# Splitting pooled columns into high and low parts: both copies of a bank before both subtracts, and a tile laid out by token

## The chip, the cores and the metric

One Trainium2 chip (trn2), one of its cores. The metric is the device time of one execution in microseconds, as the median of several runs. TensorE does the matrix products, ScalarE (ACT) copies and functions, VectorE (DVE) arithmetic on tiles, GpSimd (POOL) small odd work, SyncE (SP) issues most transfers. All of them run their own instruction lists in order and wait for one another by semaphores. PSUM, into which TensorE writes, has eight banks of 128 partitions x 512 fp32.

## The reference, cut to what matters

One layer of a trunk over 1024 latent tokens of width 1024, with 256 context tokens, all fp32. The normed and modulated tokens h are multiplied by one input projection, whose columns feed a gated linear attention and a pooling mixer. The pooling mixer takes 512 columns p = h @ w_in[:, 1568:2080], in four groups of 128 columns, group g with its own window w of 2, 4, 8 or 16 on the 16 x 64 grid of tokens:

```python
m = window_mean(window_mean(xg2, w, 2), w, 1).reshape(B, L, POOL_GROUP)
outs.append(m - xg)
y = jnp.einsum('blgc,gcd->blgd', y, w_pool)
```

Attention and pooling are joined, projected out and added to the stream; then comes a mixture of 32 experts (top group, top two of its experts), and a last norm.

## The kernel before, in words

The kernel keeps fp32 accuracy with products in the faster fp32r type: an operand is split into a high part (a ScalarE copy that rounds it to fp32r) and a low part (a VectorE subtract, operand minus high part). The helper `split` (line 196) issues these two; its copy shows as L197 and its subtract as L198 in the profile, for all operands, so the tile tells which one it is. A product is then three matmuls: high x high, high x low, low x high.

The first phase (lines 302 to 553) loads the tokens, norms and transposes them (`x_sq`, `x_rs`, `x_scale`, `x_T`: the transposes of TensorE are L332, into a bank, and ScalarE and VectorE copy half of them each to `hall`, L338 and L336), works out the modulation from `w_ada`, and computes the pooled columns. `prep` (line 395) splits a slice of `hall` into `phh` and `phl`; `wp_split` the weights into `wph` and `wpl`; `pool_mm` (line 403) adds the three products of one slice k, over four or two token tiles, into PSUM banks, one bank of 512 pooled columns for each token tile (L407, L408, L410). There are three sets of banks: `accA`, token tiles 0 to 3; `accB`, tiles 4 and 5; `accC`, tiles 6 and 7, computed in a second pass over k. When a set is complete, `pool_out` (line 412) takes its banks to SBUF: for each bank and each half m of its columns (groups 0 and 1, then 2 and 3) one split, that is one copy and one subtract of 128 partitions x 256 columns, into `pparts[m]`. The names of the profile for these tiles are `mix` and `bank`: `mix<-bank` at L197 and L198 are pool_out's instructions, eight of each for accA, four each for accB and accC.

After accA is out come the last product steps of accB, the transposes of the two context tiles (`x_T(8)`, `x_T(9)`, which use the banks of accA's first two tiles and two others), pool_out of accB, and then accC's products, among which stand `prep`, the splits of the gate weights (`wg_steps`: transfers at L249 into the two buffers `wraw`, `wgh` and `wgl`), and `row_step` (L290, sums over rows of `w_ada` that are brought into `wat`).

The order of instructions on TensorE, VectorE and ScalarE in this phase is the program's (a manual schedule); instructions from behind the phase are placed between them by the framework's scheduler, which works from its own model of time. It also derives all waits: from tiles that overlap, and from PSUM banks.

Behind the phase `box_sums` (line 559) sums over the windows on TensorE: for each group, token tile s and part j one weight tile `pparts[g // 2][:, g % 2, j, s]` (128 x 128) against constant box tables, which come through `wraw` (L601) and are rounded by ScalarE (L603, names `wvl` and `wvh`); its matmuls are L583. `box_means` (L593) scales the sums. Then follow the projections, the attention, the output projection, the router and the experts.

Of the kernel before, what the change touches and what calls it, by code (L numbers as in the profile page):

```python
# [8 lines left out]
F32 = mybir.dt.float32  # L9
F32R = mybir.dt.float32r  # L10
# [3 lines left out]
AF = mybir.ActivationFunctionType  # L14
OP = mybir.AluOpType
# [4 lines left out]
P = 128  # L20
D = 1024
NT = 8
# [110 lines left out]
def hybrid_layer(ctx, tc, x, c, ctx_in, c_ctx, w_ada, b_ada, norm1_g, w_in, w_decay, b_decay, gla_norm_g,  # L133
                 w_pool, pool_scale, w_out, norm2_g, w_rg, w_re, w_e_in, w_e_out, final_g, cst_d, inv_d, out):
    nc = tc.nc
    ve, sc, gp, te, sy = nc.vector, nc.scalar, nc.gpsimd, nc.tensor, nc.sync
# [59 lines left out]
    def split(hi, lo, src, en=ve):  # L196
        sc.activation(hi, src, AF.Copy)  # L197
        en.tensor_tensor(lo, src, hi.bitcast(F32), OP.subtract)  # L198
# [4 lines left out]
    def bank(*banks):  # L203

        turn[banks] = (turn.get(banks, -1) + 1) % len(banks)
        b = banks[turn[banks]]
        return ps.tile([P, 512], F32, name=f"bank{b}", tag=f"bank{b}")
# [12 lines left out]

    mixp = ExitStack()
    mp = mixp.enter_context(tc.tile_pool(name="mixp", bufs=1))
    pparts = [mp.tile([P, 2, 2, NT, P], F32R, name=f"mix{j}", tag=f"mix{j}") for j in range(2)]
    mixs, pcol = {}, []

    def mix_half(j):
# [75 lines left out]
    with tc.tile_pool(name="pp", bufs=2) as pp, \  # L302
# [109 lines left out]
        def pool_out(acc, half, js):  # L412
            for j in js:
                i = 4 * half + j
                for m in range(2):
                    src = acc[j][:, m * 256:(m + 1) * 256].rearrange("p (g c) -> p g c", g=2)
                    split(pparts[m][:, :, 0, i], pparts[m][:, :, 1, i], src)

        x_load(0)
        sy.dma_start(ident, cst_d[:, 0:P])  # L420
# [77 lines left out]
        for kp in range(1, 4):  # L498
# [18 lines left out]
            if kp < 3:  # L517
                prep(0, 2 * kp + 2, sc)
            else:
                pool_out(accA, 0, g4)  # L520
                prep(1, 0)
# [11 lines left out]
        x_T(8, xb)  # L533
        x_T(9, xb)
        pool_out(accB, 1, g2)
        for k in range(8):
            affine(gp, k, 1024, 1280, 1)
# [5 lines left out]
        for k in range(8):  # L543
            pool_mm(accC, 1, k, range(2, 4))
            if k < 6:
                prep(1, k + 2)
            if k in (0, 2, 4, 5):
                wg_steps[(0, 2, 4, 5).index(k)]()
            if k == 7:
                pool_out(accC, 1, range(2, 4))  # L550
            if k < 4:
                row_step()
            if k == 6:
                ada_end(7, racc, 2)
# [4 lines left out]
    def box_sums(g, box):  # L559

        down, up = BOX_REACH[g]
        tab, at = BOX_AT[g]
        accs = []
        for half in range(2):
            acc = bank(2, 3, 6, 7)
            accs.append(acc)
            todo = []
            for s in range(4 * half, 4 * half + 4):
                n = BOX_C0[g] + BOX_C[g][s]
                todo.append((s, box[2 + n // 8][:, n % 8 * P:(n % 8 + 1) * P], s, s))  # L570
            for s in range(NT):
                lo, hi = max(s - down, 4 * half), min(s + up, 4 * half + 3)
                if lo > hi:
                    continue
                near = lo - s + down
                if g == 3 and near:
                    near = 1 if hi - s < up else 6 - (hi - lo + 1)
                o = at + near * P
                todo.append((s, box[tab][:, o:o + (hi - lo + 1) * P], lo, hi))
            for n, (s, rhs, lo, hi) in enumerate(todo):  # L580
                dst = acc[:, (lo - 4 * half) * P:(hi + 1 - 4 * half) * P]
                for j in range(2):
                    te.matmul(dst, lhsT=pparts[g // 2][:, g % 2, j, s], rhs=rhs, start=(n + j == 0),  # L583
                              stop=(n == len(todo) - 1 and j == 1))
        return accs

# [33 lines left out]
    for i in range(NT):  # L620
        hs = tile_split(i)
        pg = bank(0, 1, 4)
        tokproj(pg, hs, wg)
        gs = (gpool.tile([P, 512], F32, name="gs") if i < NT - 1 else
              wst.tile([P, D], F32, name="wraw", tag="wraw", bufs=2)[:, 0:512])
        with tc.manual_schedule(engines={mybir.EngineType.Activation}):
            sc.activation(gs, pg, AF.Silu)
            if i == NT - 1:
                sc.preload_act_table_set("natural_log_exp_and_others")
        ve.tensor_tensor(gs.rearrange("p (h d) -> p h d", h=H), gs.rearrange("p (h d) -> p h d", h=H),  # L630
                         gnb[:, None, :].to_broadcast([P, H, P]), OP.mult)
        sy.dma_start(g_d[i], gs)
        if i < 7:
            for k in ((0,), (1,), (2,), (3,), (4,), (5,), (6, 7))[i]:
                ada_sum(ada_acc, 3, k)
        else:
            ada_end(5, ada_acc, 3)
        if i < 4:
            sums_g[3 - i] = box_sums(3 - i, box)
        if i == 1:  # L640
            at = mix_half(1).rearrange("p i k n -> p (i k n)")
            pcol.extend(at[:, g * D:(g + 1) * D] for g in range(4))
            box_means(3, sums_g[3])
        if 1 <= i < 4:
            box_means(3 - i, sums_g[3 - i])
        (ka_steps if i < 4 else v_steps)[i % 4]()
# [38 lines left out]
    with tc.tile_pool(name="kv", bufs=2) as kv:  # L685
# [115 lines left out]
        with tc.manual_schedule(engines={mybir.EngineType.PE}):  # L801
            k_proj(0, range(8))
            decay_in(0)
            for n in range(10):
                c = 3 if n else 6
# [513 lines left out]
    with tc.manual_schedule(engines={mybir.EngineType.PE, mybir.EngineType.DVE}):  # L1319
# [39 lines left out]
        i = NT - 1  # L1359
# [432 lines left out]
    with tc.manual_schedule(engines={mybir.EngineType.PE, mybir.EngineType.Pool, mybir.EngineType.DVE,  # L1792
# [20 lines left out]
        m = last.m  # L1813
# [105 lines left out]
```

## Time and profile before

| what | us |
|---|---|
| median of three runs | 847.03 |
| the three runs | 845.0, 847.03, 853.17 |
| the profiled execution's own time | 848.0 |
| its span in the profile | 845.9 |

The profile is of one execution. Times in rows are microseconds from the start of its span, and durations in nanoseconds where marked so. PE is TensorE's matmuls, PEld its weight loads, which overlap them; the ends of matmuls are modelled, so they are spaced more closely than their durations. A row of the timeline gives the start, the length from first start to last end, the engine, line, operation, the tile written and the tiles read, the shape and how many such instructions are merged in it; in brackets the idle time of the engine just before it and what ended that.

### The profile page before, as it was taken

To read this page: it belongs to the slowest core of one execution; us is meant where nothing else is said; L and a number is where in the kernel's file an instruction comes from. 1 tells how busy PE (TensorE), PEld (TensorE's weight loads), DVE (VectorE), ACT (ScalarE), POOL (GpSimd) and SP (SyncE) were. 2 spreads that over 40 slices of the span, in tenths; PEclk is the share of its full clock that TensorE was granted. 3 is DMA by queue.
4 is the path that set the end of the run, shared out by engine and by line. 5 is a ranking of instruction groups with operands and counts; after the bars stand their busy time and mean duration, and the time that the engine had idled before them with its cause. 6 is when DMAs were issued, how large, how long until landed. Compare 5 with 4: busy or idle time off the path is not lost. (4 is left out here: it accounts for less than half of the span.)

```text
span 845.9 us, 11767 instructions
## 1 busy us (share of the span) xinstructions
PE 742.8 (88%) x4078; PEld 502.2 (59%) x4078; DVE 428.5 (51%) x884; ACT 276.7 (33%) x525; POOL 211.1 (25%) x201
## 2 busy tenths in 40 slices
PE   4897989999999997889999564999999999997573
PEld 3675778878888985768888452434444433342232
DVE  4547856457786796754465876144223212121136
ACT  4675542344544556344443221111100101010023
POOL 2222000000000203444148655022223321221113
PEclk9999999999999998989999695899998999999688
DMA  9975774163352338564477668999999999999665
GB/s 322 300 265 175 251 255 175 58 192 131 111 171 75 138 107 311 170 200 149 138 248 240 227 217 280 289 368 370 388 349 367 348 321 351 375 357 364 205 221 200
DMA packets 78253, 206.84 MB, mean 245 GB/s; under 512 B 12515, under 2 KB 24919, under 8 KB 78193
## 3 DMA queue, kind: packets, MB, share of 16 engines
q1 hardware_dynamic: 70816, 185.45, 61.8%
q0 software_dynamic: 6624, 18.51, 9.0%
q10 hardware_dynamic: 752, 2.11, 0.9%
q8 instruction: 33, 0.54, 0.3%
q14 instruction: 28, 0.22, 0.1%
HBM read 179.68 MB, written 29.50 MB: 247 GB/s over the span
## 5 line engine op out<-in xcount | busy, mean ns | idle before, releaser
L1677 POOL DMA_INDIRECT x_d<-y,idx x30 | 43.0, 1434 | 161.5 <-DMA x_d<-y,idx 116.0
L1664 DVE SCALAR_TENSOR_TENSOR y<-bank,wtab,gtm 128x512 f32<-128x512 f32 (+1 forms) x40 | 29.5, 749 | 81.3 <-DMA x_d<-y,idx 53.5
L270 PE MATMUL bank<-woh,hh 128*128 128x512 f32 x124 | 53.3, 430 | 0.0
L271 PE MATMUL bank<-wol,hh 128*128 128x512 f32 x124 | 50.9, 410 | 0.7 <-DVE wol L198 0.7
L272 PE MATMUL bank<-woh,hl 128*128 128x512 f32 x124 | 50.8, 409 | 0.1
L1650 ACT ACTIVATE gT<-bank 128x256 f32<-128x256 f32 (+1 forms) x20 | 7.4, 376 | 132.6 <-PE bank L1648 132.6
L1624 DVE COPY hh<-bank 128x512 f32<-128x512 f32 (+1 forms) x20 | 13.4, 670 | 68.8 <-PE bank L1620 68.6
L270 PE MATMUL bank<-wkh,hh 128*128 128x288 f32 (+1 forms) x144 | 42.9, 298 | 0.0
L272 PE MATMUL bank<-wkh,hl 128*128 128x288 f32 (+1 forms) x144 | 42.0, 292 | 0.1
L271 PE MATMUL bank<-wkl,hh 128*128 128x288 f32 (+1 forms) x144 | 41.9, 291 | 0.0
L1635 PE MATMUL bank<-hall,hh 128*32 128x512 f32 (+4 forms) x156 | 40.9, 611 | 0.0
L1599 POOL DMA_INDIRECT hall<-h_d,idx x32 | 31.5, 983 | 37.2 <-PE bank L1620 28.5
L198 POOL TENSOR_TENSOR wkl<-wraw,wkh 128x512 fp32r<-128x512 f32 x4 | 6.2, 1555 | 135.1 <-ACT wkh L197 135.1
L197 ACT ACTIVATE hh<-hall 128x1024 fp32r<-128x1024 f32 x26 | 27.4, 1054 | 37.3 <-PE bank L271 33.2
L198 DVE TENSOR_TENSOR hl<-hall,hh 128x1024 fp32r<-128x1024 f32 x26 | 31.6, 1222 | 14.3 <-ACT hh L197 14.2
L1635 PE MATMUL bank<-mix,hh 128*64 128x512 f32 (+3 forms) x132 | 37.7, 600 | 0.0
L1635 PE MATMUL bank<-dS,hh 128*32 128x512 f32 (+3 forms) x88 | 37.2, 640 | 0.0
L270 PE MATMUL bank<-wvh,hh 128*128 128x512 f32 x80 | 32.0, 400 | 0.0
L271 PE MATMUL bank<-wvl,hh 128*128 128x512 f32 x80 | 31.8, 397 | 0.0
L272 PE MATMUL bank<-wvh,hl 128*128 128x512 f32 x80 | 31.6, 395 | 0.0
L1642 DVE TENSOR_TENSOR ga<-ga,bank 128x256 f32<-128x256 f32 (+1 forms) x20 | 8.4, 420 | 45.3 <-ACT ga L1641 45.2
L1620 PEld LDWEIGHTS bank<-ident,hall 128*128 128x128 f32 (+1 forms) x160 | 22.3, 211 | 15.0 <-issue 15.0
(467 smaller groups left out, 1945.5 us busy)
## 6 DMA issues: line engine op xcount, KB each, us to landing
hall<-in_w_expert_in_dram SPq DMA_DIRECT2D x25, 512.0 KB
mix<-in_w_expert_in_dram SPq DMA_DIRECT2D x25, 512.0 KB
wat<-in_w_ada_dram SPq DMA_DIRECT2D x24, 512.0 KB
dS<-in_w_expert_in_dram SPq DMA_DIRECT2D x18, 512.0 KB
wraw<-in_w_ada_dram SPq DMA_DIRECT2D x16, 512.0 KB
woh<-in_w_expert_in_dram SPq DMA_DIRECT2D x13, 512.0 KB
wraw<-in_w_in_dram SPq DMA_DIRECT2D x12, 512.0 KB
wol<-in_w_expert_in_dram SPq DMA_DIRECT2D x11, 512.0 KB
```

What stands on the lines that cost most here:

```text
L197: sc.activation(hi, src, AF.Copy)
L198: en.tensor_tensor(lo, src, hi.bitcast(F32), OP.subtract)
L270: te.matmul(dst, lhsT=ah[k], rhs=bh[k], start=(k == ends[0]), stop=False)
L271: te.matmul(dst, lhsT=ah[k], rhs=bl[k], start=False, stop=False)
L272: te.matmul(dst, lhsT=al[k], rhs=bh[k], start=False, stop=(k == ends[1]))
L1599: gp.indirect_dma_start(out=self.xg[q], out_offset=None, in_=h2_d, in_offset=ix, bounds_check=D - 1, oob_is_err=False)
L1620: te.transpose(pt[:, j * m:(j + 1) * m], self.xg[:, k // 2 * 256 + k % 2:(k // 2 + 1) * 256:2], ident[0:m, 0:m])
L1624: ve.tensor_copy(self.xT[:, 4:8], pt)
L1635: te.matmul(self.ph[q], lhsT=self.xT[:, k, q], rhs=w[:, j * 512:(j + 1) * 512], start=(k == 0), stop=(k == 7))
L1642: ve.tensor_tensor(ga, ga, self.ph[0:m, 256:512], OP.mult)
L1664: ve.scalar_tensor_tensor(y[:, ns], py[n][0:m], self.wt, gtm[0:m, ns], op0=OP.mult, op1=OP.mult)
L1677: gp.indirect_dma_start(out=x2_d, out_offset=ix, in_=y[q], in_offset=None, bounds_check=D - 1, oob_is_err=False, compute_op=OP.add)
```

## The change

For each bank, `pool_out` now issues the copies of both halves first and the subtracts of both halves after them; before, it went copy, subtract, copy, subtract. The tile `pparts[m]` is laid out by token tile, then part (high, low), then group, where it was group, part, token tile; `box_sums` takes its weight tiles at the new place. Sizes, types and the number of instructions are the same.

```diff
-    pparts = [mp.tile([P, 2, 2, NT, P], F32R, name=f"mix{j}", tag=f"mix{j}") for j in range(2)]
+    pparts = [mp.tile([P, NT, 2, 2, P], F32R, name=f"mix{j}", tag=f"mix{j}") for j in range(2)]
...
         def pool_out(acc, half, js):
             for j in js:
                 i = 4 * half + j
+                src = [acc[j][:, m * 256:(m + 1) * 256].rearrange("p (g c) -> p g c", g=2) for m in range(2)]
                 for m in range(2):
-                    src = acc[j][:, m * 256:(m + 1) * 256].rearrange("p (g c) -> p g c", g=2)
-                    split(pparts[m][:, :, 0, i], pparts[m][:, :, 1, i], src)
+                    sc.activation(pparts[m][:, i, 0], src[m], AF.Copy)
+                for m in range(2):
+                    ve.tensor_tensor(pparts[m][:, i, 1], src[m], pparts[m][:, i, 0].bitcast(F32), OP.subtract)
...
-                    te.matmul(dst, lhsT=pparts[g // 2][:, g % 2, j, s], rhs=rhs, start=(n + j == 0),
+                    te.matmul(dst, lhsT=pparts[g // 2][:, s, j, g % 2], rhs=rhs, start=(n + j == 0),
```

## Rows read from the trace of the kernel before

**Rows 1.** The page's first part: busy time, share of the span and instructions of each engine.
```profile
PE 742.8 (88%) x4078; PEld 502.2 (59%) x4078; DVE 428.5 (51%) x884; ACT 276.7 (33%) x525; POOL 211.1 (25%) x201
```

**Rows 2.** The table by stage. Columns: stretch and its length, then busy time and instructions of PE, PEld, DVE, ACT and POOL, the granted clock of TensorE (1.00 is full speed), the busy share of the 16 DMA engines, GB/s.
```profile
73.70:86.00 12.30, 8.24 (x35) 6.07 (x36) 9.14 (x20) 7.97 (x19) 4.46 (x8) 0.86 0.18 64
86.00:98.00 12.00, 12.00 (x58) 9.19 (x57) 11.36 (x13) 4.85 (x7) 0.00 (x0) 1.00 0.82 267
98.00:109.00 11.00, 9.58 (x42) 7.45 (x41) 7.22 (x13) 8.42 (x13) 0.62 (x1) 1.00 0.73 238
109.00:130.00 21.00, 19.18 (x102) 16.55 (x103) 13.48 (x15) 6.37 (x8) 0.00 (x0) 0.92 0.86 278
...
200.00:250.00 50.00, 49.93 (x306) 44.15 (x306) 40.14 (x81) 24.57 (x53) 0.00 (x0) 1.00 0.44 148
```

**Rows 3.** The waits in the stretch 73.7 to 86 us: who waited for whom, us in total, times, longest.
```profile
ACT mix L197 <- DVE mix L198: 9.3, 6, 5.5
...
PE bank L332 <- DVE mix L198: 2.5, 2, 1.9
...
DVE mix L198 <- ACT mix L197: 2.2, 5, 0.5
PE bank L407 <- ACT phh L197: 2.0, 2, 1.6
```

**Rows 4.** The timeline of 66 to 76 us, on ScalarE, VectorE and TensorE.
```profile
68.36 0.37 ACT L197 ACTIVATE mix<-bank 128x256 fp32r<-128x256 f32 x1
...
69.21 1.28 DVE L290 SCALAR_TENSOR_TENSOR racc<-wat,cT,racc 128x1024 f32<-128x1024 f32 x1 [1.76 <-DMA wat<-in_w_ada_dram]
...
73.75 0.42 DVE L198 TENSOR_TENSOR mix<-bank,mix 128x256 fp32r<-128x256 f32 x1
74.20 0.66 ACT L197 ACTIVATE mix<-bank 128x256 fp32r<-128x256 f32 x2 [5.47 <-DVE mix L198]
74.62 0.76 DVE L198 TENSOR_TENSOR mix<-bank,mix 128x256 fp32r<-128x256 f32 x2 [0.45 <-ACT mix L197]
75.19 0.63 PE L332 MATMUL bank<-ident,xs 128*128 128x128 f32 x4 [1.91 <-DVE mix L198]
```

**Rows 5.** The timeline of 75 to 90.5 us, on the same engines.
```profile
75.41 0.66 ACT L197 ACTIVATE mix<-bank 128x256 fp32r<-128x256 f32 x2 [0.55 <-DVE mix L198]
...
76.39 2.03 PE L332 MATMUL bank<-ident,xs 128*128 128x128 f32 x12 [0.58 <-DVE mix L198]
...
78.60 0.48 DVE L606 MEMSET gs<- 128x512 f32 x1 [0.82 <-PE bank L332]
78.77 0.80 PE L407 MATMUL bank<-wph,phh 128*128 128x512 f32 x1 [0.34 <-ACT phh L197]
79.00 0.36 DVE L198 TENSOR_TENSOR mix<-bank,mix 128x256 fp32r<-128x256 f32 x1
...
80.64 0.64 PE L410 MATMUL bank<-wph,phl 128*128 128x512 f32 x2
81.11 0.39 PE L407 MATMUL bank<-wph,phh 128*128 128x512 f32 x1
...
81.68 0.41 DVE L198 TENSOR_TENSOR mix<-bank,mix 128x256 fp32r<-128x256 f32 x1
...
83.74 0.42 DVE L198 TENSOR_TENSOR mix<-bank,mix 128x256 fp32r<-128x256 f32 x1 [0.45 <-ACT mix L197]
...
84.28 0.50 PE L407 MATMUL bank<-wph,phh 128*128 128x512 f32 x1 [1.65 <-ACT phh L197]
...
85.37 0.73 PE L410 MATMUL bank<-wph,phl 128*128 128x512 f32 x2
```

**Rows 6.** Instructions by tile and by line, with the least, median and largest duration in ns, first and last start in us, and the shapes: pool_out's copies and subtracts; the copy of line 711 and, below it, what it waited for (us, times); the VectorE sum of line 298.
```profile
L197 ACT ACTIVATE mix<-bank x16: 366/384/392, 68.4 to 101.5; 128x256 fp32r<-128x256 f32 x16
L198 DVE TENSOR_TENSOR mix<-bank,mix x16: 361/416/425, 73.8 to 102.8; 128x256 fp32r<-128x256 f32 x16
...
L711 ACT ACTIVATE kvb<-bank x10: 365/384/385, 172.0 to 280.7; 128x256 f32<-128x256 f32 x10
...
  DVE aext L710: 7.6, 8
...
L298 DVE TENSOR_TENSOR bg<-bank,bg x1: 417/417/417, 98.3 to 98.3; 128x256 f32<-128x256 f32 x1
```

**Rows 7.** The timeline of 75 to 90.5 and 90 to 104 us, the gate weights' instructions on VectorE, ScalarE and SyncE's queue (SPq).
```profile
85.24 1.21 DVE L198 TENSOR_TENSOR wgl<-wraw,wgh 128x1024 fp32r<-128x1024 f32 x1
...
86.48 0.39 SPq L249 DMA_DIRECT2D wraw<-in_w_in_dram  x1
...
89.97 1.21 DVE L198 TENSOR_TENSOR wgl<-wraw,wgh 128x1024 fp32r<-128x1024 f32 x1
90.07 1.06 ACT L197 ACTIVATE wgh<-wraw 128x1024 fp32r<-128x1024 f32 x1 [1.86 <-DMA wraw<-in_w_in_dram]
...
91.21 0.38 SPq L249 DMA_DIRECT2D wraw<-in_w_in_dram  x1
...
96.06 1.06 ACT L197 ACTIVATE wgh<-wraw 128x1024 fp32r<-128x1024 f32 x1 [4.40 <-DMA wraw<-in_w_in_dram]
```

**Rows 8.** The timeline of 104 to 150 us, TensorE's first box sums.
```profile
108.92 1.00 PE L583 MATMUL bank<-wvl,mix 128*128 128x128 f32 x7 [1.42 <-ACT wvl L603]
...
110.74 6.26 PE L583 MATMUL bank<-wvl,mix 128*128 128x128 f32 x28 [0.82 <-ACT wvl L603]
```

## The prediction

> **What bounds the kernel now.** I read first the busy line of the page: TensorE is busy for 742.8 of 845.9 us [rows 1], so the end can only come earlier where TensorE stands idle, or runs slowly, and gets something for it. Next the table by stage [rows 2]. The stretch 73.7 to 86.0 us is the poor one: TensorE busy 8.24 of 12.30 us at a granted clock of 0.86, VectorE 9.14, the DMA engines at a share of 0.18. That is the stage in which the first two sets of pooled banks are split. Behind it TensorE is full in 86 to 98 and (49.93 of 50) in 200 to 250; between lie shorter gaps at 98 to 109 and 109 to 130. A microsecond saved in the poor stretch therefore shifts full work, and stays saved unless one of the two later gaps grows by it.
>
> Then the waits of that stretch [rows 3]. ScalarE's copies waited 9.3 us, six times, for VectorE's subtract, at most 5.5 us in one go; VectorE waited 2.2 us in five waits for ScalarE's copy; TensorE waited 2.5 us for the subtract (a bank that a transpose wants) and 2.0 us for ScalarE's high part of the next operand.
>
> Last the order of time. I call A0, A1 the copies of a bank's two high parts (groups 0 and 1, then 2 and 3) and S0, S1 the subtracts for its low parts. A0 of the first bank runs at 68.36, then ScalarE does nothing until 74.20, when A1 starts right behind S0 (73.75 + 0.42) [rows 4]. A1 and S0 share no data: they write different tiles and read different halves of the bank. Yet A1 waits, and the next bank's A0 does not (A1 and A0 run as a pair of 0.66 us, ahead of S1 at 74.62). So what is kept apart is two engines on one bank. The same shows far away: the copy of line 711 waited eight times, 7.6 us, for the VectorE instruction of line 710, which reads other columns of its bank [rows 6]. Each bank is thus a chain A0, S0, A1, S1, with one bank per 1.21 us (74.20 to 75.41) [rows 4, 5].
>
> The Trainium skill, "PSUM — Partial Sum Buffer" (section "PSUM bank collisions raise a hardware error"), says that two engines must not be on the same bank and partitions at once, reads against reads included, and that different banks are free. The two waits above agree. The rule speaks in part against this change: S0 will now have to wait for A1 too, some 0.3 us (half of a 0.66 us pair), which by itself would make each set of banks later, not earlier, where VectorE follows close on ScalarE.
>
> **The change part by part.** No instruction is added or removed, and each engine's own list keeps its order: ScalarE A0, A1, A0, A1 ..., VectorE S0, S1, S0, S1 .... No DMA is issued in this step, and nothing is moved past the queues of SP or POOL. What moves is the waiting: S0 now waits for A1, A1 no longer waits for S0.
>
> *Cost of the instructions.* High and low parts are now written as one run of 256 columns in place of two of 128. A copy of 128x256 out of a bank into one run (line 711) has a median of 384 ns, the A's 384; a subtract with one run (line 298) 417, the S's 416 [rows 6]. So zero. TensorE's weight tile is 128 columns in one run in both layouts: zero as well; no row of before shows the new stride between such tiles, and as each load still reads one run I bound it at 0 on either side.
>
> *First set, four banks.* ScalarE is free to run all eight copies at 68.36 to 71.2 (four pairs of 0.66 us, and links), then the high parts of the next two operands, which today start only after the last A1. VectorE can't start sooner: it stands behind a sum that waited for a transfer until 69.21, and reaches S0 at 73.75 [rows 4]. From there eight subtracts in pairs of 0.76 [rows 4] take 3.0 us and end at 76.8; today the last one ends at 79.36 (79.00 + 0.36) [rows 5]. In that time VectorE also cleared a tile, 0.48 us at 78.60, after a wait of 0.82 for TensorE's transposes [rows 5]. If the clearing keeps its place ahead of the next low part, it follows the transposes; if not, it costs its 0.48 behind them. So the gain of VectorE here is 1.2 (it must wait for the transposes) to 2.5 us (it need not).
> TensorE: the first transposes wait for S1 of bank 0, the rest for S1 of bank 1. S1 now ends at 74.5 and 75.3; with the 0.19 us that lay between its end and the transpose (75.00 to 75.19) the second group starts at 75.45 in place of 76.39 and, at its 2.03 us, ends at 77.5 in place of 78.4 [rows 4, 5]. The first product of the third set, at 78.77 today because of ScalarE's high part, then starts at about 77.55: 1.2 us earlier.
>
> *Second set, two banks.* Today S0 at 81.68, last S1 ends at 84.16 (83.74 + 0.42): 2.48 us [rows 5]. Four subtracts back to back: 1.5 us. Gain 1.0, on top of the 1.2 to 2.5: VectorE is 2.2 to 3.5 us ahead. TensorE waits 1.65 us before 84.28 for a high part that ScalarE could make only after the last A1 [rows 5]; ScalarE will be early. What comes late next is VectorE's low part of the same operand: today used at 85.37, then 82.2 to 83.2. TensorE, from 77.55, needs 2.3 us for the first product step (78.77 to 81.1 today) and 1.4 for the next, is at the third at 81.3, and wants its low part at 82.3. So it is there 2.2 to 3.1 us ahead of today. I take 2.9 us, nearer the upper end: of VectorE's idle time here (12.30 - 9.14 = 3.16 us [rows 2]) nearly all is those links.
>
> *Clock.* In 78.77 to 80.64 four products start 0.47 us apart [rows 5], in 86 to 98 58 fill 12.0 us [rows 2], 0.21 apart; the granted clock of 0.86 says that part of this stretch ran at the lower of the two levels, 1.2 instead of 2.4 GHz. With shorter gaps some of it may go: 0 to 1 us; I take 0.1, as the gap of 1.9 us ahead of the transposes shrinks by only 0.5.
>
> *Third set, two banks, behind 98 us.* Nothing waits for it before the box sums at 108.92, and TensorE has other products to run. The added wait of S0 is 0.33 us (half a pair of copies) for each of two banks on VectorE; ScalarE frees earlier by about as much, and behind it stand the copies of the box tables. I bound it at -1 to +0.6 and take 0.
>
> *Does the advance reach the end?* The third set's stage lives on the chain by which weights of the gate projection come in: a buffer comes free with a VectorE subtract (85.24 + 1.21), its transfer is issued at 86.48 and used at 90.07; the second is freed at 91.18 (89.97 + 1.21), issued at 91.21 and used at 96.06 [rows 7]. Both issues hang on VectorE, so they move with it. The box tables use the same two buffers and end the gaps at 108.92 (1.42 us) and 110.74 (0.82 us) [rows 8]; they move too. With a DMA share of 0.18 in the poor stretch and 0.73 to 0.86 after it [rows 2] there is room to take the transfers earlier. Later stages follow TensorE.
>
> Sum: 2.9 + 0.1 + 0 = 3.0 us. The profiled execution took 848.0 us (span 845.9), so 845.0; it lay 1.0 above the median of the three runs, 847.03. Forecast 844.0 us.
>
> **Rivals.**
> *The advance is taken back at the box tables.* If transfers issued 3 us earlier land no earlier (they then share the engines with others; a table issued for the gap at 108.92 waits behind them), that gap grows from 1.42 us by up to the whole advance. For it: ScalarE waited there on transfers twice over, and the two uses of the buffers took 3.6 and 4.85 us from issue, so landing times vary by more than 1 us [rows 7]. Against: share 0.18 just before. Left 0 to 1 us: 846.5.
> *All idle time of the place goes.* TensorE's idle 4.06 us in the poor stretch (12.30 - 8.24), the two gaps of 2.24 us and 1 us of clock: 7.3 us, 839.7. Against: the transposes still wait for VectorE.
> *Slower: the order of the other work is written anew.* The lists of ScalarE, VectorE and TensorE hold instructions of later stages in between (the clearing at 78.60 is one: it stands ahead of the last S1 and made it wait). With other waits these may be placed elsewhere. One that needs a transfer, put ahead of the products, holds its engine until that has landed: 4.40 us before the copy at 96.06 is such a wait, harmless there [rows 7]. From one such block on it decides: 847.0 - 3.0 + 4.4 = 848.4 us; two make 852.8.
> *The change doesn't do what it says.* If the next bank's copy still waits for this bank's subtracts (through the tile that both write), each bank is A pair, link, S pair, link: 0.66 + 0.05 + 0.76 + 0.03 = 1.50 against 1.21 us. Five such steps: 1.5 us lost, 848.5. Against it: high and low parts of a bank now lie next to each other, apart from the next bank's, and A0 already runs ahead of the previous bank's S1.
>
> **How the numbers follow.** Forecast (a gain of 2 to 4.5 us) 0.45; taken back at the tables 0.2; all idle time 0.13; order anew 0.15; doesn't do what it says 0.07. The range runs from the full-idle case, 839.7 with 0.7 for its own spread, to the order case with a block and a half, 850.5: 839.0 to 850.5. About 1%, 8.5 us, is what a measurement of this kernel can tell from no change (its three runs lie 8 us apart). Faster by more than that needs the full-idle case and a kinder order besides: 0.11; slower by more, three blocks: 0.08; within, 0.81.
>
> **What would show it.** Right: the waits of ScalarE's A for VectorE's S are gone (9.3 to under 1 us); eight S in one row from about 73.75; the first product of the third set near 77.5; the wait for the high part at 84.28 gone; the gate weights' transfers issued near 83.5 and 88; the box sums near 106. The table copies waiting longer on transfers at an unmoved 108.9 would show the first rival, a new wait of over 3 us ahead of a product on VectorE or ScalarE the third, A waiting for the previous bank's S1 the fourth. The forecast is wrong if VectorE does not gain 2 us by 84, or if the expert stage moves by itself.

## The result, and the profile after

The changed kernel took 840.23 us, the median of 18 runs (835.62 to 845.97); the kernel before 848.41 (18 runs, 837.09 to 857.16). The ratio is 0.9934, 95% interval [0.9909, 0.9959]: 5.6 us less of 848.4, between 3.5 and 7.7. The ratios, here and below, leave out runs over 1.5% above the fastest of their kernel (six of these 18 of before; of order alone, among others, one of 1998.87 us), so this one isn't the quotient of the two medians, 0.990. The profiled execution of after took 844.05 us, span 842.0. The forecast was 844.0 us and a gain of 3.0. In after, lines behind 417 have moved: the copies of pool_out are L417 and its subtracts L419, the box sums L585, the box tables' rounding L605, the clearing L608.

The page's first part and the table by stage, columns as in [rows 1, 2], to be held against those rows; the busy time of TensorE is much the same in all (743.9 us, 742.8 before), so what this execution gained is idle time (842.0 - 743.9 = 98.1 us, 103.1 before):

```profile
PE 743.9 (88%) x4078; PEld 502.8 (60%) x4078; DVE 431.0 (51%) x884; ACT 276.1 (33%) x525; POOL 217.1 (26%) x201
```

```profile
73.70:86.00 12.30, 12.30 (x57) 9.49 (x55) 12.30 (x18) 7.76 (x14) 10.28 (x8) 1.00 0.39 121
86.00:98.00 12.00, 12.00 (x58) 9.04 (x57) 9.39 (x16) 4.76 (x8) 0.62 (x1) 1.00 0.90 298
98.00:109.00 11.00, 8.42 (x35) 6.51 (x34) 5.26 (x6) 5.88 (x7) 0.00 (x0) 0.76 0.48 150
109.00:130.00 21.00, 21.00 (x124) 18.87 (x123) 14.05 (x18) 7.33 (x10) 1.08 (x2) 0.96 0.87 272
...
200.00:250.00 50.00, 49.92 (x319) 44.81 (x319) 38.22 (x73) 24.03 (x54) 0.00 (x0) 1.00 0.43 143
```

The poor stretch, 73.7 to 86 us, is full: TensorE busy 12.30 us with 57 matmuls where it had 8.24 us with 35, and the granted clock is 1.00 in place of 0.86. TensorE's idle time over 73.7 to 130 us, 7.30 us before, is 2.58, all of it at 98 to 109. The stretches are fixed in time, though, and 2.34 us of the move are no work of the change: the first subtract starts at 71.41 in place of 73.75. For 1.76 us of it the reason is that in this execution the row of `w_ada` for the sum ahead of the subtracts had landed, while [rows 4] had to wait for it; the rest was there ahead of that sum. In the twelve profiles of this document that sum starts anywhere from 66.87 to 69.69 us, in either order of pool_out; a second execution of the changed kernel, after again below, has the wait too (2.06 us). There the first subtract starts at 74.24, nearly as in before, and the same stretch reads:

```profile
73.70:86.00 12.30, 10.87 (x54) 8.59 (x54) 12.30 (x23) 6.78 (x13) 8.40 (x8) 1.00 0.35 107
```

So like for like TensorE's idle time there went from 4.06 to 1.43 us, not to nothing. From here on places are told by their distance from the first subtract of pool_out.

The waits in 73.7 to 86 us (who waited for whom, us, times, longest; this is the whole answer). The copies wait for no subtract, here or in 66 to 86 us. One wait of [rows 3] is left in part and lies ahead of this stretch, since the stage starts earlier: TensorE waits 1.35 us for the subtract, in one go, before its transposes at 72.31 (2.5 us in two before):

```profile
POOL hall L391 <- ACT hall L338: 4.1, 1, 4.1
ACT wgh L197 <- DMA wraw<-in_w_in_dram: 3.1, 1, 3.1
PEld bank L410 <- DVE phl L198: 1.0, 3, 0.4
ACT hall L338 <- PE bank L332: 0.5, 1, 0.5
```

The timeline of after on VectorE, ScalarE, TensorE and SP's issues, 66 to 85 us and two later places, to be held against [rows 4, 5, 7, 8]:

```profile
66.87 1.29 DVE L290 SCALAR_TENSOR_TENSOR racc<-wat,cT,racc 128x1024 f32<-128x1024 f32 x1
67.73 2.29 ACT L417 ACTIVATE mix<-bank 128x256 fp32r<-128x256 f32 x8
71.41 2.73 DVE L419 TENSOR_TENSOR mix<-bank,mix 128x256 fp32r<-128x256 f32 x8
72.31 2.16 PE L332 MATMUL bank<-ident,xs 128*128 128x128 f32 x16 [1.35 <-DVE mix L419]
74.22 0.48 PE L407 MATMUL bank<-wph,phh 128*128 128x512 f32 x1
74.56 1.21 ACT L417 ACTIVATE mix<-bank 128x256 fp32r<-128x256 f32 x4
...
76.47 1.40 DVE L419 TENSOR_TENSOR mix<-bank,mix 128x256 fp32r<-128x256 f32 x4
78.53 0.73 PE L410 MATMUL bank<-wph,phl 128*128 128x512 f32 x2
79.64 0.38 SPq L249 DMA_DIRECT2D wraw<-in_w_in_dram  x1
...
84.81 0.38 SPq L249 DMA_DIRECT2D wraw<-in_w_in_dram  x1
...
93.49 0.48 DVE L608 MEMSET gs<- 128x512 f32 x1
101.62 1.75 PE L585 MATMUL bank<-wvl,mix 128*128 128x128 f32 x11 [1.38 <-ACT wvl L605]
104.57 7.47 PE L585 MATMUL bank<-wvl,mix 128*128 128x128 f32 x28 [1.20 <-ACT wvl L605]
```

ScalarE copies four banks in one row of 2.29 us, VectorE subtracts them in one row of 2.73. The chain of 1.21 us per bank is gone, and the transposes go in one row of 16 where there were 4, a wait, and 12. The clearing, which stood ahead of the last subtract [rows 5], now stands at 93.49.

From the first subtract to four places behind it, in us; "third low part" is the product that uses the third step's low part (85.37 before, 78.53 after), "gate transfer" the first issue at L249 shown:

| | before | after |
|---|---|---|
| last of eight subtracts ends | 5.61 | 2.73 |
| first product of the third set | 5.02 | 2.81 |
| third low part | 11.62 | 7.12 |
| gate transfer | 12.73 | 8.23 |
| first box sum | 35.2 | 30.2 |

### The profile page after: what moved, and what is told of

Same layout as the page of the kernel before. It is cut to its first block, busy times and chain, and to the rows that moved or that the text cites. A ratio compares the mean times of both kernels' runs of the same rounds, so it can differ in the third digit from the quotient of the medians.

```text
span 842.0 us, 11776 instructions
## 1 busy us (share of the span) xinstructions
PE 743.9 (88%) x4078; PEld 502.8 (60%) x4078; DVE 431.0 (51%) x884; ACT 276.1 (33%) x525; POOL 217.1 (26%) x201
## 5 line engine op out<-in xcount | busy, mean ns | idle before, releaser
L198 DVE TENSOR_TENSOR hl<-hall,hh 128x1024 fp32r<-128x1024 f32 x26 | 31.6, 1220 | 18.6 <-ACT hh L197 18.5
L1601 POOL DMA_INDIRECT hall<-h_d,idx x32 | 31.4, 982 | 36.8 <-PE bank L1622 28.2
```

The lines of the kernel that those rows point to most:

```text
L1601: gp.indirect_dma_start(out=self.xg[q], out_offset=None, in_=h2_d, in_offset=ix, bounds_check=D - 1, oob_is_err=False)
```

## The experiments

Each ratio is against the kernel before, run on the same chip in the same rounds. Of theories I held, with the forecast: copies and subtracts on one bank wait for each other, whatever columns they read, so the old order makes a chain of them. Against it stood the layout, a chain by pairs of halves, the clearing, and kinder lists further on.

**Order or layout.** The change taken apart: the new order in the old tile, and the new tile under the old order.

```diff
# new order, old layout (against before)
                 for m in range(2):
-                    src = acc[j][:, m * 256:(m + 1) * 256].rearrange("p (g c) -> p g c", g=2)
-                    split(pparts[m][:, :, 0, i], pparts[m][:, :, 1, i], src)
+                    sc.activation(pparts[m][:, :, 0, i], src[m], AF.Copy)
+                for m in range(2):
+                    ve.tensor_tensor(pparts[m][:, :, 1, i], src[m], pparts[m][:, :, 0, i].bitcast(F32), OP.subtract)
# new layout, old order (against before)
-                    split(pparts[m][:, :, 0, i], pparts[m][:, :, 1, i], src)
+                    split(pparts[m][:, i, 0], pparts[m][:, i, 1], src)
```

> The new order of copies and subtracts with the old layout of their tile. Theory (the wait of two engines on one bank is the whole of it): ScalarE waits under 1 us for the subtracts, the eight subtracts of the first set run in one row of 2.7 to 3.0 us, the first product of the third set starts 4 to 6 us ahead of the kernel before measured from the first subtract's place, time 0.990 to 0.997 of before, as the full change. Rival (the layout is needed, because a high part of the next bank and a low part of this one lie in strides that cross in the old tile): the copies of the next bank wait for the subtracts again, some 1.5 us per bank, time 0.998 to 1.003.

> The new layout with the old order. Theory: as before, 0.998 to 1.003, ScalarE's copies waiting 8 to 11 us for subtracts in the stage, first copy pair stopped until the first subtract is done; it also shows whether the 1.76 us wait for a row of w_ada ahead of the first subtract, which the profile of the changed kernel lacks, comes again in a second profile of the old order (then the first subtract is at 73 to 74 us; by chance alone it would lie anywhere in 71 to 74). Rival (layout): 0.990 to 0.996.

Measured: the order alone 0.9915 [0.9875, 0.9955], the layout alone 1.003 [0.9996, 1.0063]. The timeline of the order alone has the rows of after, at the same distances (2.82 us from the first subtract to the first product, 8.25 to the gate transfer):

```profile
68.90 2.29 ACT L417 ACTIVATE mix<-bank 128x256 fp32r<-128x256 f32 x8
73.00 2.73 DVE L419 TENSOR_TENSOR mix<-bank,mix 128x256 fp32r<-128x256 f32 x8
75.82 0.48 PE L407 MATMUL bank<-wph,phh 128*128 128x512 f32 x1
```

The layout alone keeps the old pairs, and the copies' waits for the subtracts (8.2 us in six in 66 to 88 us; 9.3 in [rows 3]):

```profile
72.36 0.42 DVE L198 TENSOR_TENSOR mix<-bank,mix 128x256 fp32r<-128x256 f32 x1
72.81 0.66 ACT L197 ACTIVATE mix<-bank 128x256 fp32r<-128x256 f32 x2 [3.75 <-DVE mix L198]
```

The order makes the gain; the layout does nothing that can be measured. In the old layout, too, eight copies ran in one row with no wait for a subtract, so high and low parts that lie apart made no copy wait.

**Is it the bank, and is it the clearing?** One kernel keeps the old pairing of copy and subtract but takes all first halves, then all second halves (the loop over m outside that over j). A chain by pairs would stay; a wait by bank falls on the four second copies at once. The other is the kernel before with the clearing moved behind the third set.

```diff
# halves outside (against before)
-            for j in js:
-                i = 4 * half + j
-                for m in range(2):
+            for m in range(2):
+                for j in js:
+                    i = 4 * half + j
# clearing late (against before): these two lines from behind the box tables' loop to behind the third set's products and pool_out
+        wdec_in = gpool.tile([P, 512], F32, name="gs").rearrange("p (h d k) -> p h d k", h=H, d=2)
+        ve.memset(wdec_in, 0.0)
```

> The old pairing, each copy followed by its subtract, but all first halves of a set's banks before all second halves, so that copy and subtract alternate over different banks. Theory (what waits is a bank shared by two engines, not the pairing): the four A0 run in one row without a wait, then one wait of ScalarE, until the first subtract is done (4 to 6 us), and after it no more; eight subtracts in one row of 2.7 to 3.1 us (one clearing may stand between them); the first bank is free 1.1 us later than in the change, so the time lies between: 0.992 to 0.999 of before. Rival (each copy waits for the subtract before it in the program, whatever the bank): 1.2 us per pair as before, 0.999 to 1.004.

> The kernel before, with the clearing of the decay weights' tile taken out of the middle of the first set's subtracts and put behind the third set, as the changed kernel has it; the ten small transfers into that tile follow it on the queue. Theory (the bank's wait): a gain of 0.5 to 1.3 us at most (the 0.48 us and its wait of 0.82), ScalarE still waits 8 to 11 us, time 0.997 to 1.002. Rival (what the change gained is the new place of that work and of its transfers): 0.990 to 0.995 with the copies still waiting.

Measured: halves outside 1.0036 [1.0005, 1.0066], clearing late 0.9978 [0.995, 1.0006]. The timeline with halves outside:

```profile
68.56 1.19 ACT L197 ACTIVATE mix<-bank 128x256 fp32r<-128x256 f32 x4
73.10 2.73 DVE L198 TENSOR_TENSOR mix<-bank,mix 128x256 fp32r<-128x256 f32 x8
73.55 1.38 ACT L197 ACTIVATE mix<-bank 128x256 fp32r<-128x256 f32 x4 [3.81 <-DVE mix L198]
74.99 1.94 PE L332 MATMUL bank<-ident,xs 128*128 128x128 f32 x16 [2.38 <-DVE mix L198]
```

Four first copies run without a wait, though each has its subtract still open; the fifth, on the first bank again, waits 3.81 us until that bank's subtract is done (73.10 + 0.42). So the wait hangs on the bank, not on the pair, and after it the eight subtracts take 2.73 us as in after. The first product then comes 3.58 us and the gate transfer 9.76 behind the first subtract (before 5.02 and 12.73): a local advance of 3.0 us at the transfer. Yet the time is no better: 1.0036 missed the theory's 0.992 to 0.999 and lies where the rival put it, though the rival's reason, a wait by pairs, is refuted by the rows. A part of the advance is lost further down the same trace, VectorE's rows first:

```profile
127.00 1.22 DVE L198 TENSOR_TENSOR wvl<-wraw,wvh 128x1024 fp32r<-128x1024 f32 x1 [2.71 <-ACT wvh L197]
128.15 1.28 DVE L593 TENSOR_TENSOR mix<-bank,inv 128x512 f32<-128x512 f32 x2
...
128.89 2.33 PE L583 MATMUL bank<-wvl,mix 128*128 128x128 f32 x16 [2.70 <-DVE mix L593]
```

The scaling of box sums (L593) stands on VectorE behind a value-weight subtract that waits 2.71 us for ScalarE's copy, and TensorE, which wants the bank, waits 2.70 us for it. The last box sums start 69.8 us behind the first subtract, as before (70.05). I took this for the third rival, an order of other work that takes an advance back, and tried it.

**The same pairing under another order of the other work.** Both edits of the last pair together, called the combined kernel below; the clearing's place leads to other lists behind it.

> The kernel with all first halves ahead of all second halves, with the clearing moved behind the third set. The engines' lists come out otherwise behind the phase: VectorE's scaling of the first box sums now stands ahead of the value weights' subtract that waits for a transfer, as in the changed kernel. In the halves kernel alone the first box sum started 31.4 us behind the first subtract (35.2 in the kernel before), yet the last one 69.8 behind it (70.05), and TensorE stood 2.7 us for that scaling. Theory (the advance of the pooled columns' stage was there and the new lists of the box stage took it back): first box sum again 30 to 32 us behind the first subtract, no wait of over 1 us for the scaling, last box sum 63 to 67 us behind, time 0.990 to 0.996 of before. Rival (the pairing by halves is itself no gain, because banks are freed later): 0.998 to 1.004 again.

Measured: 0.9888 [0.9842, 0.9935]. The subtracts are those of halves outside, and the scaling stands ahead of the value weights, with a wait of its own for the sums alone:

```profile
71.57 2.74 DVE L198 TENSOR_TENSOR mix<-bank,mix 128x256 fp32r<-128x256 f32 x8
73.46 2.77 PE L332 MATMUL bank<-ident,xs 128*128 128x128 f32 x16 [2.25 <-DVE mix L198]
...
121.28 1.29 DVE L595 TENSOR_TENSOR mix<-bank,inv 128x512 f32<-128x512 f32 x2 [1.36 <-PE bank L585]
```

The gate transfer comes 9.35 us behind the first subtract, much as in halves outside, but the last box sums at 66.9 against 69.8. So the advance of the first stage is not enough, and where the other work stands made the difference: the clearing alone gave about 2 us of 846 (0.9978, interval up to 1.0006), so it isn't what made 0.9888 by itself. That it is the lists of the box stage is shown in part only. They account for 2.9 us at the last box sums; the two ratios lie 1.5%, some 12 us, apart, and the two profiled executions took nearly the same (847.57 and 846.88 us), so the rest isn't seen in them.

**The clearing, from the other side.** After, with the clearing put right behind pool_out of accB.

```diff
# clearing early (against after): the two lines of the clearing from lines 607 and 608 to behind pool_out(accB, ...)
+        wdec_in = gpool.tile([P, 512], F32, name="gs").rearrange("p (h d k) -> p h d k", h=H, d=2)
+        ve.memset(wdec_in, 0.0)
```

> The changed kernel with the clearing of the decay weights' tile put back early, right behind the second set's subtracts, so that its ten small transfers (0.66 us of SP's time each) stand again ahead of and between the gate weights' transfers on SP's queue. Theory (removing the wait is the whole of it): eight subtracts in a row of 2.7 us, first product of the third set 2.8 us behind the first subtract as in the change, and the time as the change, 0.990 to 0.995. Rival (the early gain is only kept because that other work moved out of the way): the local distance is still 2.8 us, but the gate weights' transfers are issued 2 to 4 us later, the box sums start at 104 us or later, time 0.996 to 1.003.

Measured: 0.9935 [0.9901, 0.9968], with the subtracts in one row and the clearing at 6.51 us behind the first:

```profile
73.24 2.73 DVE L419 TENSOR_TENSOR mix<-bank,mix 128x256 fp32r<-128x256 f32 x8
...
79.75 0.48 DVE L544 MEMSET gs<- 128x512 f32 x1
...
82.95 0.53 SPq L249 DMA_DIRECT2D wraw<-in_w_in_dram  x1
```

The transfer is 1.5 us later than in after (9.71 against 8.23). The ratio is that of after above, 0.9934; after again, run in the same rounds as this kernel, gives 0.9893 [0.9859, 0.9928]. The two intervals overlap, so the clearing's new place is no part of the gain that can be told from nothing, but a part of some 0.4%, which clearing late (0.9978) would allow as well, isn't excluded.

**What is left in the way.** Three on one chip with the one above: a first box table that comes through a third buffer, so that the gap ahead of the box sums shrinks; ScalarE's copy of line 711 (713 in after) put ahead of the VectorE reads of its bank; and after itself once more.

```diff
# third buffer (against after)
-        t = wst.tile([P, D], F32, name="wraw", tag="wraw", bufs=2)
+        t = kvw.tile([P, D], F32, name="inv") if j == 0 else wst.tile([P, D], F32, name="wraw", tag="wraw", bufs=2)
# copy first (against after): this line moved ahead of VectorE's two reads
             sc.activation(kvb[:, 512:768], s["pk"][:, 0:256], AF.Copy)
```

> The changed kernel with a third staging buffer for the box tables: the first table comes through the tile of the pooled means' factors, not through the two buffers that the gate weights hold. Theory (part of the advance is lost at the tables, where TensorE waits 2.6 us in the changed kernel and runs at a granted clock of 0.76): the waits for ScalarE's tables fall under 1.5 us and the first box sum starts 1 to 3 us earlier, time 0.986 to 0.993 of before. Rival (the tables are not the limit; VectorE and the later weights are): box sums earlier, but their end and the time as the change, 0.990 to 0.996.

> The changed kernel with the same reordering in the one other place where two engines read one bank in turns: ScalarE's copy of line 711 now stands ahead of VectorE's two reads of the bank. Theory (a removed wait is worth something only where TensorE waits for it): the copy's 7.6 us of waits for VectorE go, VectorE's reads start 0.4 us later each, TensorE is full there (49.92 of 50 us), so the time is the change's, 0.990 to 0.996. Rival (each such wait costs on its own): 2 to 4 us faster than the change, 0.985 to 0.990.

> The changed kernel itself, on the chip of the other three. 0.990 to 0.996; the first product of the third set 2.8 us behind the first subtract, as in its first profile; the place of the first subtract (71.4 us in that profile, 73.75 in the kernel before) shows by how much the row of w_ada ahead of it comes and goes by chance.

Measured: third buffer 0.9925 [0.9893, 0.9958], copy first 0.9884 [0.985, 0.9917], after again 0.9893 [0.9859, 0.9928]: one time for all three, within their intervals. After again itself lies just under its 0.990 to 0.996, so these rounds gave more than the first ones. Copy first, against before, falls into its rival's range (0.985 to 0.990), but what it adds to the change has to be read against after again: 0.9884 against 0.9893, nothing.

With the third buffer the first box sums come 28.3 us behind the first subtract in place of 30.2, and the wait ahead of them is 0.94 us; then TensorE waits 2.67 us for the next table. The gap only moved by one table:

```profile
100.66 3.08 PE L585 MATMUL bank<-wvl,mix 128*128 128x128 f32 x19 [0.94 <-ACT wvl L605]
...
106.41 4.68 PE L585 MATMUL bank<-wvl,mix 128*128 128x128 f32 x28 [2.67 <-ACT wvl L605]
```

Copy first takes away ScalarE's eight waits for VectorE, 7.9 us in after (7.6 in [rows 6]), and puts two of VectorE, 2.5 us, in their place; nothing is gained that can be measured, and TensorE is full over most of that stretch (49.92 of 50 us in 200 to 250). It is the same conflict as that of the change, on one bank by two engines, at a place where the engine that waits isn't the bound. In both kernels, the waits of the second engine's line (the groups by line):

```profile
  DVE aext L712: 7.9, 8
```

```profile
  ACT kvb L711: 2.5, 2
```

After again is the execution with the late row of `w_ada`; its first subtract starts at 74.24, and the distances are those of after all the same (2.81, 8.24, 30.0 us):

```profile
69.69 1.28 DVE L290 SCALAR_TENSOR_TENSOR racc<-wat,cT,racc 128x1024 f32<-128x1024 f32 x1 [2.06 <-DMA wat<-in_w_ada_dram]
...
74.24 2.73 DVE L419 TENSOR_TENSOR mix<-bank,mix 128x256 fp32r<-128x256 f32 x8
...
104.25 1.75 PE L585 MATMUL bank<-wvl,mix 128*128 128x128 f32 x11 [1.15 <-ACT wvl L605]
107.06 4.69 PE L585 MATMUL bank<-wvl,mix 128*128 128x128 f32 x28 [1.05 <-ACT wvl L605]
```

**The first set alone.** The new order only for token tiles 0 to 3; the second and third set go copy, subtract, copy, subtract again, in the new layout.

```diff
# first set alone (against after)
                 for m in range(2):
                     sc.activation(pparts[m][:, i, 0], src[m], AF.Copy)
-                for m in range(2):
+                    if i >= 4:
+                        ve.tensor_tensor(pparts[m][:, i, 1], src[m], pparts[m][:, i, 0].bitcast(F32), OP.subtract)
+                for m in range(2 if i < 4 else 0):
                     ve.tensor_tensor(pparts[m][:, i, 1], src[m], pparts[m][:, i, 0].bitcast(F32), OP.subtract)
```

> The changed kernel with the new order in the first set's four banks only; the second and third set go copy, subtract, copy, subtract as before. By the terms of the sum the first set carries 1.2 to 2.5 us of the gain and the second set 1.0, seen at the gate weights' first transfer behind the first subtract (12.7 us in the kernel before, 8.2 in the change): theory 9.2 to 10.5 us here, time 0.993 to 0.998 of before. Rival (it is the second set, on which ScalarE's next high parts wait, that carries it): 11.5 us or more, 0.997 to 1.002. Unless the lists behind the phase fall badly, which the last box sum's distance from the first subtract shows (over 69 us).

Measured: 0.9976 [0.9945, 1.0007]. The first set runs as in after, the second waits as before, and the gate transfer is issued 10.07 us behind the first subtract:

```profile
74.03 2.74 DVE L421 TENSOR_TENSOR mix<-bank,mix 128x256 fp32r<-128x256 f32 x8
...
79.53 0.66 ACT L417 ACTIVATE mix<-bank 128x256 fp32r<-128x256 f32 x2 [1.97 <-DVE mix L419]
...
81.70 0.50 PE L407 MATMUL bank<-wph,phh 128*128 128x512 f32 x1 [1.86 <-ACT phh L197]
...
84.10 0.39 SPq L249 DMA_DIRECT2D wraw<-in_w_in_dram  x1
```

Of the 4.5 us of local advance (12.73 to 8.23) the first set gives 2.7 and the second 1.8: TensorE's wait for ScalarE's high part, 1.65 us in [rows 5], stays here (1.86) and goes with the second set. The clearing stands early again in this kernel, with its small transfers ahead of the gate transfer on SP, so some 0.2 of the 1.8 may be theirs.

The kernels side by side, distances from the first subtract in us (the profiled execution of order alone took 847.46 us, more than any other of its runs but the one named above, so its later places are left out):

| kernel | gate transfer | first box sum | last box sums | ratio |
|---|---|---|---|---|
| before | 12.73 | 35.2 | 70.05 | 1 |
| layout alone | 13.37 | 34.7 | 70.8 | 1.003 |
| clearing late | 12.47 | 34.6 | 70.8 | 0.9978 |
| halves outside | 9.76 | 31.4 | 69.8 | 1.0036 |
| first set alone | 10.07 | 32.9 | 68.4 | 0.9976 |
| clearing early | 9.71 | 31.6 | 65.1 | 0.9935 |
| after | 8.23 | 30.2 | 65.9 | 0.9934 |
| order alone | 8.25 | – | – | 0.9915 |
| third buffer | 8.25 | 28.3 | 64.0 | 0.9925 |
| halves outside, clearing late | 9.35 | 30.8 | 66.9 | 0.9888 |
| after again | 8.24 | 30.0 | 62.8 | 0.9893 |
| copy first | 8.23 | 30.9 | 66.9 | 0.9884 |

Where the last box sums lie over 68 us behind the first subtract, the ratio can't be told from 1 or is above it; where they lie under 67, it is 0.7 to 1.2% under. The order within the faster half isn't told by the table, and the place is a sign, not a shown cause: the profiled executions that it is read from don't part in time as the ratios do (clearing early 845.39 us and the combined kernel 846.88; layout alone 845.33 and first set alone 845.76).

## Why the prediction was right, and where its sizes were off

The direction, the place and the range held: 840.23 us lies in 839.0 to 850.5, near its lower end. The mechanism is shown, by the order alone and by halves outside: two engines on one bank wait for each other, and grouping the accesses by engine undoes it. The size was low: 3.0 us forecast, 5.6 [3.5, 7.7] measured. Going through its steps:

- *Copies and subtracts cost the same.* Right: the 16 subtracts have a median of 412 ns (416 before), the 16 copies 394 (384 before). Here are the groups by tile, with least, median and greatest ns:

```profile
L417 ACT ACTIVATE mix<-bank x16: 366/394/447, 67.7 to 92.1; 128x256 fp32r<-128x256 f32 x16
L419 DVE TENSOR_TENSOR mix<-bank,mix x16: 410/412/417, 71.4 to 93.0; 128x256 fp32r<-128x256 f32 x16
```

- *First set.* Forecast for VectorE 1.2 to 2.5 us, measured 5.61 - 2.73 = 2.9. Eight subtracts in a row take 2.73 and not 3.0 us (they start some 0.33 apart, not at 0.76 for a pair), and the wait for the transposes did not stay, since the clearing that caused it went to 93.49. For the first product 1.2 forecast, 5.02 - 2.81 = 2.2 measured: the 16 transposes start 0.90 us behind the first subtract and run in 2.16 us without a break, where I had them end at 77.5, that is 3.75 behind it.
- *Second set, to the third low part.* This is the step that failed, in size: 2.2 to 3.1 us, 2.9 taken, against 11.62 - 7.12 = 4.5 us measured, the first set's 2.2 and the clock of the next point included. I had let VectorE's low part set the place, with TensorE at the pace of before. Of the 4.5 us some 3.1 are idle time of TensorE behind the first subtract: before 1.44 + 0.58 + 0.34 + 1.65 = 4.0 us [rows 4, 5], after the 0.9 us ahead of the transposes. The other 1.4 us are pace: the 16 transposes took 0.63 + 2.03 = 2.66 us before and 2.16 after, and the first products the 0.9 us of the next point. VectorE's four subtracts do run in one row of 1.40 us (1.5 forecast), but they start at 5.06 us behind the first in place of 7.93.
- *Clock, 0.1 us.* Too low. The first products of the third set start 0.25 us apart in after (four spaces from 74.22 to 75.23) and 0.47 in [rows 5] (78.77 to 80.64); for four spaces that is 0.9 us, near my upper bound of 1. Granted were 1.00 in after and 0.86 in [rows 2], and not by chance of one profile: in 73.7 to 86 us before, layout alone and clearing late have 0.86, the seven kernels and executions with the new order in the first set all 1.00. So the clock came with the change. What it is worth by itself shows where the waits are alike and the clock isn't: halves outside (1.00) runs its 16 transposes in 1.94 us after a wait of 2.38, the combined kernel (0.86) in 2.77 after one of 2.25.
- *Third set, 0.* Not measured by itself. First set alone has the old order in the third set too, but the gate transfer, where it is 1.8 us later than after, comes ahead of that set; at the first box sum it is 2.7 us later (32.9 against 30.2), so up to 0.9 us could be the third set's.
- *The advance reaches the weights' chain.* Right, and whole: 4.5 us at the gate transfer, 5.0 at the first box sum. Behind the box sums 4.2 us remain in after (70.05 to 65.9) and 7.3 in the second execution of it (62.8).

The rivals. *Taken back at the box tables:* not as forecast, since the first box sum keeps 5.0 us; what the tables cost stays, waits of 1.38 and 1.20 us against 1.42 and 0.82 [rows 8]. *All idle time goes:* in part. Of the poor stretch's idle time some 3 of 4 us went, and the 1 us of clock nearly whole; the transposes still wait for VectorE, as I had held against it, and the gaps at the tables did not go. The measured 5.6 us lie above the forecast's own case (2 to 4.5), whose upper end is what the stage itself gained (4.5), and below this rival's 7.3; the median of 840.23 us is next to this rival's 839.7. *The order of other work written anew:* borne out by the two kernels with halves outside, which differ in the clearing's place and the lists behind it: with nearly one advance at the gate transfer (9.76 and 9.35) one is no faster than before and one is 1.1% faster. Through which list is shown for 2.9 us of it only. In the changed kernel it fell on the good side; no row of before told on which, so that part was luck. *The change doesn't do what it says:* fell; no copy waited for another bank's subtract.

A page of the Trainium skill is weighed in the prediction: "PSUM — Partial Sum Buffer", section "PSUM bank collisions raise a hardware error", which says that two engines must not be on the same bank at once, reads included, and that different banks are free. Halves outside agrees: 3.81 us of wait on the bank that VectorE still has to read, and none for the first copies of the three other banks. That the first subtract now waits for both copies, which I held against the change, cost nothing: VectorE came 1.4 us after ScalarE had finished (67.73 + 2.29 to 71.41).

What stays open. The gain of 5.6 us has an interval, 3.5 to 7.7, that holds the 4.5 to 5.0 us of the first stage; the 9.1 us (6.1 to 12.0) in the rounds of after again, 1.07% of 848.18, are more. Single profiles differ more than that further on: the product of the pooled means with `w_pool` (line 898, 896 in before) starts 235.3 us behind the first subtract in after, 228.1 in after again and 237.4 in before. From these no later place can be named. What the runs do show is the granted clock over the whole span: its mean is 0.940 over the 18 runs of after and 0.941 in the rounds of after again, and 0.936 to 0.937 for before in the rounds of the experiments. Within the runs of before 0.01 of it goes with 4 to 6 us, so by an estimate from these numbers 1 to 3 us of the gain go with the clock. Whether it rose because of the kernel's shorter waits isn't shown.

## What to carry to other kernels

Where two engines read one PSUM bank in turns, give each engine all its accesses of that bank in one go; what can be gained is the chain of waits. Here it counted in a stage where TensorE stood idle for it; the same conflict at line 711, where TensorE is mostly full, was worth nothing that could be measured. Price a stretch that speeds up by everything in it that was paced by the waits, the engine behind and the clock included, not by the one link you remove. And an advance of a few us has to get through the lists behind it: look which in-order list has an instruction that waits for a transfer ahead of one that TensorE needs.

## What the runs showed of the hardware

The same program had two clocks in the same stage. In 98 to 109 us the granted clock was 0.76 in after, so part of it at 1.2 GHz, and 28 box sums took 7.47 us; in after again it was 1.00, 2.4 GHz throughout, and they took 4.69 us. The waits of TensorE just ahead of them hardly differ: 1.38 and 1.20 us against 1.15 and 1.05. Here is that stretch in after again:

```profile
98.00:109.00 11.00, 8.80 (x46) 6.76 (x45) 6.50 (x7) 6.00 (x8) 0.00 (x0) 1.00 0.64 202
```

In the poor stretch all seven profiles with the new order in the first set had 1.00, and the three with the old pairs 0.86. But the waits alone don't tell it: halves outside, after a wait of 2.38 us ahead of the transposes, had 1.00, and the combined kernel, after 2.25, had 0.86. This is the row of halves outside:

```profile
73.70:86.00 12.30, 10.82 (x54) 8.52 (x54) 12.24 (x22) 9.11 (x19) 7.32 (x8) 1.00 0.25 78
```

So from one profile a clock term can be bounded, not foretold.

Also new to me: copies of 128x256 that need no one run 0.27 us apart (eight in 2.29), though one takes 0.37 to 0.39; eight subtracts take 2.73, 0.33 apart, at 0.41 each. A sum of single lengths is too long by a third for the copies (3.1) and by a fifth for the subtracts (3.3).
